# Latent attention: TensorE takes a pair's products in a written order, the plain fp32 ones together

## The chip, the cores and the metric

The kernel runs on one core of a Trainium2 chip. The metric is the device time of one execution in microseconds (us), lower is better. All engines of the core work at once, each in its own instruction order, and wait for one another through semaphores: TensorE (PE in the profile; PEld is its loading of weights), VectorE (DVE), ScalarE (ACT), GpSimd (POOL) and SyncE (SP), which here issues the loads.

## The reference

A trunk of two layers over 256 tokens of width 2048. The first mixes tokens by a gated product within chunks, the second by latent attention; both attend to 256 memory tokens beside it and end in a gated ConvFFN. The change lies in the latent attention of the second layer. Cut to what matters, for a block of 128 query positions:

```python
qa = jnp.einsum('bqhn,rhn->bqhr', qn, w_uk)
s = (jnp.einsum('bqhr,bkr->bhqk', qa, c_kv)
     + jnp.einsum('bqhp,bkp->bhqk', qr, k_rope)).astype(jnp.float32) * scale
s = jnp.where(k_pos[None, :] <= q_pos[:, None], s, -jnp.inf)
p = jax.nn.softmax(s, axis=-1).astype(c_kv.dtype)
o_lat = jnp.einsum('bhqk,bkr->bqhr', p, c_kv)
return jnp.einsum('bqhr,rhv->bqhv', o_lat, w_uv)
```

There are 12 heads. A score is the sum of a product over 128 "nope" dimensions and one over 64 rotary dimensions; the first query block sees 128 keys and the second 256. A value product follows the softmax, and then the output projection `w_out`, which also takes the four heads of memory attention.

## The kernel before

**Number formats.** Most products keep fp32 accuracy in three fp32r products: an operand is split into a high part (an fp32r copy by ACT) and a low part (the difference, by DVE), and `three` (lines 600 to 604) multiplies high by high, low by high and high by low. Where both operands are used plainly, one fp32 product is issued instead. In the profile an fp32 product of 128x128 weights shows as two matmul records, an fp32r product as one; a transposition of a 128x128 block is one record, on plain fp32 data too.

**Stages.** `layer_b` builds the latent tiles, then the value tiles of all heads (`vh`, `vl` split, `v1` plain), and then walks through six pairs of heads in the loop at line 1296. Round i makes the queries and keys of pair i (`queries`, `keys`: fp32r, weights split from `raw` into `whi` by ACT and `wlo` by DVE) and gives the rotary part to POOL (`rotary`, tiles `rm`, `rn`, then `qr` split by ACT and DVE). It then takes, in the program's text:

- `turn` for both heads of pair i-2: three transpositions of the probabilities `p` each, into one PSUM tile; ACT and DVE split the first 256 columns into `pT` (high, low) and ACT copies the last 128 into `pl`;
- `mturn` for a memory head: four transpositions;
- `scores` for pair i-1: for each query block (`qb` 0 with 128 keys, 1 with 256) one PSUM bank, into which three fp32r rotary products (`krz`, `qr`; both heads side by side) and then the two heads' fp32 products (`qn` and `kn`, which lie in `scratch`) are summed; `softmax` follows on DVE and ACT for each head;
- `attend` for both heads of pair i-2: three fp32r products of `pT` and `exact`, one fp32 product of `pl` and `scratch`, and a split of the result into `mainhl`;
- `mout` and `mscores` for memory heads, fp32r throughout (`mpT`, `rest`, `exact`).

The last pair's scores, and the transpositions and value products of the last two pairs, stand as hooks between chunks of `w_out`'s first quarter (`hooks`, line 1318). Below, round i is one pass of that loop, and the first and second head are the two of its pair i-2.

**What sets the order.** The program is built with a scheduler that moves instructions on each engine by a timeline of its own; the text above is its input, not its result. A block of code under `manual_schedule(engines=...)` keeps its instructions in written order on the engines it names; before the change, this part has none. PSUM tiles come from one pool of eight banks (`psum`), so that a new tile waits until the readers of the tile that last had its bank are done. All loads go through SP's queue in program order.

Of the kernel before, what the change touches and what calls it, by code (L numbers as in the profile page):

```python
# [16 lines left out]
P = 128  # L17
D = 2048
S = 256
# [55 lines left out]
class Kernel:  # L75
# [1003 lines left out]
    def layer_b(self):  # L1079
# [9 lines left out]
        with tc.tile_pool(name="lb", bufs=1) as lb:  # L1089
# [138 lines left out]
            def scores(pr):  # L1228
                bank = [self.psum() for _ in range(2)]
                for qb in range(2):  # L1230
                    n = P * (qb + 1)
                    q = [qr[pr][:, i * S + qb * P : i * S + (qb + 1) * P] for i in range(2)]
                    both = bank[qb][:, : 2 * n].rearrange("p (j k) -> p j k", j=2)
                    self.three(both, q, [k[:, :, :n] for k in krz], True, False)
                    for j in range(2):
                        mm(both[:, j, :], qn[pr][:, j, qb * P : (qb + 1) * P], kn[pr][:, j, :n], start=False, stop=j == 1)  # L1236
                for j in range(2):
                    softmax(2 * pr + j, [bank[qb][:, j * P * (qb + 1) : (j + 1) * P * (qb + 1)] for qb in range(2)])
# [21 lines left out]
            def turn(h):  # L1260
# [4 lines left out]
                pT, last = self.tmp(lp, [P, 576], "pT", 2, F32R)[:, 13 : 13 + 512], self.tmp(lp, [P, P], "pl", 2)  # L1265
                self.split(pT, acc[:, :S])
                nc.scalar.activation(last, acc[:, S : 3 * P], AF.Copy)
                pa[h] = pT, last

            def attend(h):  # L1270
                pT, last = pa.pop(h)
                o = self.psum()
                cols = slice(h * P, (h + 1) * P)
                self.three(o[:, :S], (vh[:, cols], vl[:, cols]), (pT[:, :S], pT[:, S:]), True, False)
                mm(o[:, P:S], v1[:, cols], last, start=False, stop=True)
                self.split(hl[:, h, :], o[:, :S])
# [280 lines left out]
```

## Time and profile before

| | |
|---|---|
| median of 3 runs | 2030.38 us (2029.91 to 2031.34) |
| span of the profiled execution, first to last instruction | 2027.8 us |
| granted TensorE clock, mean | 0.999 |
| PE busy | 2017.2 us (99%) |
| DVE busy | 1618.2 us (80%) |
| ACT busy | 1167.1 us (58%) |
| POOL busy | 112.8 us (6%) |
| chain that ended last, by engine | PE 99% |

The page gives the span of the profiled execution and no device time of its own beside it; the timed runs of the same kernel lie 2.1 to 3.5 us above that span, the median 2.58 us. Starts are counted from the beginning of the span. The latent attention's pairs stand between about 1163 and 1243 us of it. In the timeline a row is one instruction or a run of equal ones: its start, its length, the engine, line, operation, output and inputs, shape and count, and in brackets the idle time just before it and what ended it. Matmuls are pipelined, so their lengths overlap, and the distance between the starts of neighbours tells how fast PE goes.

### The profile page before, as it was taken

How to read it: one execution, taken by the hardware profiler on the slowest of the kernel's cores; microseconds unless marked ns; L12 is line 12 of the kernel's file. 1: busy time of each engine (PE TensorE's matmuls, PEld its weight loads, DVE VectorE, ACT ScalarE, POOL GpSimd, SP SyncE). 2: the span in 40 equal slices, each digit the busy share in tenths (PEclk: the TensorE clock that was granted, in tenths of full speed). 3: DMA queues.
4: the chain of work that ended last, by engine and by line, in shares of the span. 5: the costliest groups of instructions: out<-in, count | busy, mean ns of one | idle time of the engine just before them, and what ended most of it. 6: DMA issues, size and time to landing. Idle time of an engine off the chain costs nothing.

```text
span 2027.8 us, 38053 instructions
## 1 busy us (share of the span) xinstructions
PE 2017.2 (99%) x15136; PEld 1912.3 (94%) x15136; DVE 1618.2 (80%) x2433; ACT 1167.1 (58%) x1675; POOL 112.8 (6%) x169
## 2 busy tenths in 40 slices
PE   9999999999999999999999999999999999999998
PEld 8989999999889999899989999999988999889996
DVE  6866766778898788987878786777889878898787
ACT  6754744545565555655566675455566555565565
POOL 0000013100000000000002141400000000000000
PEclk9999999999999999999999999999999999999999
DMA  8876556688657676577656634568865767657764
GB/s 255 234 216 181 166 193 195 192 209 259 208 177 218 198 240 199 179 216 246 187 179 187 183 113 162 190 196 210 257 205 181 219 192 246 196 177 219 241 206 145
DMA packets 248263, 409.24 MB, mean 202 GB/s; under 512 B 71502, under 2 KB 78996, under 8 KB 248084
## 3 DMA queue, kind: packets, MB, share of 16 engines
q1 hardware_dynamic: 247892, 406.27, 65.4%
q8 instruction: 118, 1.93, 0.4%
q14 instruction: 61, 0.50, 0.1%
q10 hardware_dynamic: 192, 0.54, 0.1%
HBM read 400.46 MB, written 2.10 MB: 199 GB/s over the span
## 4 chain that ended last, share of the span: by engine, by line
PE 99%; DVE 0%; ACT 0%; issue 0%; ACTq 0%
PE ps L157 22%; PE ps L158 22%; PE ps L160 22%; PE ps L796 7%; PE ps L797 7%; PE ps L795 7%; PE ps L189 2%; PE ps L190 2%; PE ps L191 2%; PE ps L524 1%; PE ps L406 0%; PE ps L604 0%; PE ps L602 0%; PE ps L603 0%; PE ps L1236 0%; PE ps L1024 0%
## 5 line engine op out<-in xcount | busy, mean ns | idle before, releaser
L118 ACT ACTIVATE whi<-raw 128x1024 fp32r<-128x1024 f32 x484 | 512.7, 1061 | 513.1 <-PE ps L158 373.6
L119 DVE TENSOR_TENSOR wlo<-raw,whi 128x1024 fp32r<-128x1024 f32 x484 | 599.0, 1241 | 246.6 <-ACT whi L118 244.1
L157 PE MATMUL ps<-xhl,whi 128*128 128x256 f32 x3264 | 763.1, 277 | 0.0
L158 PE MATMUL ps<-xhl,whi 128*128 128x256 f32 x3264 | 761.5, 276 | 0.0
L158 PEld LDWEIGHTS ps<-xhl,whi 128*128 128x128 f32 x3264 | 612.8, 188 | 0.5
L157 PEld LDWEIGHTS ps<-xhl,whi 128*128 128x128 f32 x3264 | 612.7, 188 | 0.6
L160 PE MATMUL ps<-xhl,wlo 128*128 128x256 f32 x3264 | 436.6, 276 | 0.0
L160 PEld LDWEIGHTS ps<-xhl,wlo 128*128 128x128 f32 x3264 | 400.5, 188 | 0.0
L710 DVE TENSOR_TENSOR wlo<-raw,whi 128x1024 fp32r<-128x1024 f32 x112 | 134.3, 1220 | 31.5 <-ACT whi L709 30.3
L796 PE MATMUL ps<-wlo,h 128*128 128x512 f32 x404 | 157.3, 390 | 0.0
L797 PE MATMUL ps<-whi,h 128*128 128x512 f32 x404 | 157.2, 389 | 0.0
L709 ACT ACTIVATE whi<-raw 128x1024 fp32r<-128x1024 f32 x112 | 115.7, 1055 | 53.1 <-PE ps L158 37.3
L795 PE MATMUL ps<-whi,h 128*128 128x512 f32 x404 | 128.8, 390 | 0.0
L157 PE MATMUL ps<-mainhl,whi 128*128 128x256 f32 x512 | 119.7, 277 | 0.0
L158 PE MATMUL ps<-mainhl,whi 128*128 128x256 f32 x512 | 119.3, 276 | 0.0
L890 ACT ACTIVATE c<-a,cT 128x256 f32<-128x256 f32 x176 | 99.7, 592 | 32.2 <-DVE a L237 30.2
L709 ACT ACTIVATE whi<-xs 128x1024 fp32r<-128x1024 f32 x52 | 53.8, 1059 | 87.3 <-DVE xs L757 73.1
L158 PEld LDWEIGHTS ps<-mainhl,whi 128*128 128x128 f32 x512 | 96.0, 188 | 0.0
L157 PEld LDWEIGHTS ps<-mainhl,whi 128*128 128x128 f32 x512 | 95.9, 188 | 0.0
L795 PEld LDWEIGHTS ps<-whi,h 128*128 128x128 f32 x404 | 75.8, 188 | 15.7
L797 PEld LDWEIGHTS ps<-whi,h 128*128 128x128 f32 x404 | 75.8, 188 | 15.7
L796 PEld LDWEIGHTS ps<-wlo,h 128*128 128x128 f32 x404 | 75.9, 188 | 15.4
(378 smaller groups left out, 2896.6 us busy)
## 6 DMA issues: line engine op xcount, KB each, us to landing
raw<-in_w_ffn_up SPq DMA_DIRECT2D x352, 512.0 KB, 4.4
raw<-in_w_ffn_down SPq DMA_DIRECT2D x126, 512.0 KB, 4.5
raw<-in_w_out SPq DMA_DIRECT2D x64, 512.0 KB, 3.9
raw<-in_w_in_a SPq DMA_DIRECT2D x56, 512.0 KB, 4.2
gate<-in_w_ffn_down SPq DMA_DIRECT2D x38, 512.0 KB, 4.6
raw<-in_w_mem_kv SPq DMA_DIRECT2D x31, 512.0 KB, 4.8
sums<-in_w_ffn_down SPq DMA_DIRECT2D x48, 256.0 KB, 7.1
raw<-in_w_in_b SPq DMA_DIRECT2D x16, 512.0 KB, 4.1
```

What stands on the lines that cost most here:

```text
L118: nc.scalar.activation(hi[:, :n], raw[:, :n], AF.Copy)
L119: nc.vector.tensor_tensor(lo[:, :n], raw[:, :n], hi[:, :n].bitcast(F32), ALU.subtract)
L157: mm(acc[:, :S], wh, x[:, :S], start=first, stop=False)
L158: mm(acc[:, :S], wh, x[:, S:], start=False, stop=False)
L160: mm(acc[:, :S], wl, x[:, :S], start=False, stop=last)
L189: mm(acc, xh, wh, start=first, stop=False)
L709: self.behind(self.nc.scalar.activation(hi, w, AF.Copy))
L710: self.behind(self.nc.vector.tensor_tensor(lo, w, hi.bitcast(F32), ALU.subtract))
L795: mm(o, xh, wh, start=start, stop=False)
L796: mm(o, xh, wl, start=False, stop=False)
L797: mm(o, xl, wh, start=False, stop=stop)
L890: nc.scalar.activation(c, a, AF.Identity, scale=w(2), bias=w(3))
```

## The change

It does four things. `scores` writes the four fp32 products of a pair first, for both query blocks, and the six rotary fp32r products behind them. `turn` copies `pl` before it splits `pT`. `attend` takes two heads: both heads' three fp32r products, then both fp32 products, then both splits. And in the loop, `turn`, `mturn`, `scores` and `attend` stand in one block that keeps PE in written order; `mout` and `mscores` stand outside it, and so do the hooks, whose `scores` and `attend` calls are only passed another way.

```diff
             def scores(pr):
                 bank = [self.psum() for _ in range(2)]
+                both = [bank[qb][:, : 2 * P * (qb + 1)].rearrange("p (j k) -> p j k", j=2) for qb in range(2)]
                 for qb in range(2):
                     n = P * (qb + 1)
+                    for j in range(2):
+                        mm(both[qb][:, j, :], qn[pr][:, j, qb * P : (qb + 1) * P], kn[pr][:, j, :n], start=j == 0, stop=False)
+                for qb in range(2):
                     q = [qr[pr][:, i * S + qb * P : i * S + (qb + 1) * P] for i in range(2)]
-                    both = bank[qb][:, : 2 * n].rearrange("p (j k) -> p j k", j=2)
-                    self.three(both, q, [k[:, :, :n] for k in krz], True, False)
-                    for j in range(2):
-                        mm(both[:, j, :], qn[pr][:, j, qb * P : (qb + 1) * P], kn[pr][:, j, :n], start=False, stop=j == 1)
+                    self.three(both[qb], q, [k[:, :, : P * (qb + 1)] for k in krz], False, True)
...
                 pT, last = self.tmp(lp, [P, 576], "pT", 2, F32R)[:, 13 : 13 + 512], self.tmp(lp, [P, P], "pl", 2)
+                nc.scalar.activation(last, acc[:, S : 3 * P], AF.Copy)
                 self.split(pT, acc[:, :S])
-                nc.scalar.activation(last, acc[:, S : 3 * P], AF.Copy)
                 pa[h] = pT, last
 
-            def attend(h):
...
+            def attend(*heads):
+                outs = [(h, self.psum(), slice(h * P, (h + 1) * P), *pa.pop(h)) for h in heads]
+                for h, o, cols, pT, last in outs:
+                    self.three(o[:, :S], (vh[:, cols], vl[:, cols]), (pT[:, :S], pT[:, S:]), True, False)
+                for h, o, cols, pT, last in outs:
+                    mm(o[:, P:S], v1[:, cols], last, start=False, stop=True)
+                for h, o, *_ in outs:
+                    self.split(hl[:, h, :], o[:, :S])
...
+                with tc.manual_schedule(engines={mybir.EngineType.PE}):
+                    if i >= 2:
+                        turn(2 * i - 4)
+                        turn(2 * i - 3)
+                        mturn(i - 2)
+                    if i >= 1:
+                        scores(i - 1)
+                    if i >= 2:
+                        attend(2 * i - 4, 2 * i - 3)
                 if i >= 2:
-                    turn(2 * i - 4)
-                    turn(2 * i - 3)
-                    mturn(i - 2)
-                if i >= 1:
-                    scores(i - 1)
-                if i >= 2:
-                    attend(2 * i - 4)
-                    attend(2 * i - 3)
                     mout(i - 2)
...
-                2: calls(attend, pairs[0]),
+                2: [lambda: attend(*pairs[0])],
                 3: calls(turn, pairs[1]),
-                5: calls(attend, pairs[1]),
+                5: [lambda: attend(*pairs[1])],
```

No instruction is added or removed on any engine, and SP's and POOL's orders stay as they were. Line numbers shift: a pair's fp32 score product is L1236 before and L1234 after, a head's transposition L1264 and L1265, its fp32 value product L1275 and L1276.

The first place is PE in round 2, from the transpositions to the value products. `ident,p` are the heads' transpositions and `ident,mp` the memory head's; `krz,qr` are the rotary products, `scratch` alone the fp32 score products, `pT,exact` the value products in fp32r and `pl,scratch` those in fp32; a number behind a name is the tile's. Before:

```order
L645 MATMUL ps_13848<-ident,mp_13713 128x128 x4
L602 MATMUL ps_13856<-krz_12346,qr_13626 128x256
...
L604 MATMUL ps_13856<-krz_12347,qr_13626 128x256
L1236 MATMUL ps_13856<-scratch 128x128 x2
L602 MATMUL ps_13857<-krz_12346,qr_13626 128x512
...
L1236 MATMUL ps_13857<-scratch 128x256 x2
L602 MATMUL ps_13888<-pT_13834,exact 128x256
L603 MATMUL ps_13888<-pT_13834,exact 128x256
L602 MATMUL ps_13895<-pT_13843,exact 128x256
L603 MATMUL ps_13895<-pT_13843,exact 128x256
L604 MATMUL ps_13888<-pT_13834,exact 128x256
...
L1275 MATMUL ps_13888<-pl_13835,scratch 128x128
```

And with the change:

```order
L645 MATMUL ps_13856<-ident,mp_13719 128x128 x4
L1234 MATMUL ps_13864<-scratch 128x128 x2
L1234 MATMUL ps_13865<-scratch 128x256 x2
L602 MATMUL ps_13864<-krz_12346,qr_13629 128x256
...
L604 MATMUL ps_13864<-krz_12347,qr_13629 128x256
L602 MATMUL ps_13865<-krz_12346,qr_13629 128x512
...
L602 MATMUL ps_13896<-pT_13842,exact 128x256
L603 MATMUL ps_13896<-pT_13842,exact 128x256
L604 MATMUL ps_13896<-pT_13842,exact 128x256
L602 MATMUL ps_13897<-pT_13851,exact 128x256
...
L1276 MATMUL ps_13896<-pl_13843,scratch 128x128
L1276 MATMUL ps_13897<-pl_13852,scratch 128x128
```

The fp32 score products moved up to the transpositions, and the two fp32 value products stand next to each other. The first head's third value product (L604, which reads the low part of `pT`) moved from fifth to third of the value products, ahead of the second head's first two.

The second place is PE in `w_out`'s first quarter, where the last pair's scores stand (`mainhl,whi` and `mainhl,wlo` are `w_out`'s products). Before, the scores of the two query blocks follow each other:

```order
L1236 MATMUL ps_14561<-scratch 128x128 x2
L602 MATMUL ps_14562<-krz_12346,qr_14401 128x512
L603 MATMUL ps_14562<-krz_12346,qr_14401 128x512
L604 MATMUL ps_14562<-krz_12347,qr_14401 128x512
L1236 MATMUL ps_14562<-scratch 128x256 x2
```

With the change, this is where the second bank begins:

```order
L1234 MATMUL ps_14579<-scratch 128x128 x2
L602 MATMUL ps_14579<-krz_12346,qr_14416 128x256
...
L604 MATMUL ps_14579<-krz_12347,qr_14416 128x256
L157 MATMUL ps_14545<-mainhl_13326,whi_14630 128x256
...
L157 MATMUL ps_14548<-mainhl_13326,whi_14630 128x256
...
L1234 MATMUL ps_14580<-scratch 128x256 x2
...
L1265 MATMUL ps_14611<-ident,p_14502 128x128 x3
```

Between the two banks stand now twelve products of `w_out` (the first and the last are shown), and the second bank's products come ahead of the transpositions instead of following the first bank at once. The second bank (`ps_14562` before, `ps_14580` after) takes the place in PSUM of a value product's output of round 5 (`ps_14504` before, `ps_14521` after), eight tiles earlier, and waits until that one is split.

The third place is DVE in round 5, which makes the low part of that split (`mainhl`); `md` and `p` belong to the softmax of pair 4. Before:

```order
L1250 TENSOR_SCALAR md_14494<-md_14494 128x2
L246 TENSOR_TENSOR mainhl_13326<-ps_14504,mainhl_13326 128x256
L1255 RECIPROCAL md_14484<-md_14484 128x2
...
L1257 TENSOR_SCALAR p_14495<-p_14495,md_14494 128x256
L246 TENSOR_TENSOR mainhl_13326<-ps_14511,mainhl_13326 128x256
```

And with the change:

```order
L1251 TENSOR_SCALAR md_14511<-md_14511 128x2
L1256 RECIPROCAL md_14501<-md_14501 128x2
...
L1258 TENSOR_SCALAR p_14512<-p_14512,md_14511 128x256
L246 TENSOR_TENSOR mainhl_13326<-ps_14521,mainhl_13326 128x256
L246 TENSOR_TENSOR mainhl_13326<-ps_14522,mainhl_13326 128x256
```

The first head's split moved from ahead of the softmax's last steps to behind them, and ACT's high part moved likewise. Over the whole attention, PE goes from a plain fp32 instruction (a product or a transposition) to an fp32r one 30 times before and 15 times after: in round 1 two and one, in each of rounds 2 to 5 five and two, in the hooks eight and six.

More of the change, by code (lines that the diff above doesn't have):

```diff
@@ L1265, in turn @@
                 pT, last = self.tmp(lp, [P, 576], "pT", 2, F32R)[:, 13 : 13 + 512], self.tmp(lp, [P, P], "pl", 2)
+                nc.scalar.activation(last, acc[:, S : 3 * P], AF.Copy)
                 self.split(pT, acc[:, :S])
-                nc.scalar.activation(last, acc[:, S : 3 * P], AF.Copy)
                 pa[h] = pT, last
-            def attend(h):
[L1271 to L1276, printed above, removed]
+            def attend(*heads):
[6 more added lines that the diff above has]
+                    self.split(hl[:, h, :], o[:, :S])
             parts = {}
```

## The prediction

> **What bounds the kernel.** I read the page first, then the list of what PE waited for, then a table by stage, and last the timelines of PE, DVE and ACT in the latent attention.
>
> ```profile
> span 2027.8 us, 38053 instructions
> PE 99%; DVE 0%; ACT 0%; issue 0%; ACTq 0%
> ```
>
> ```profile
> PE ps L491 <- DVE ones L288: 1.1, 1, 1.1
> PE ps L604 <- DVE pT L246: 0.2, 1, 0.2
> PE ps L796 <- DVE wlo L710: 0.2, 1, 0.2
> ```
>
> ```profile
> core 0: us, PE busy (x) PEld busy (x) DVE busy (x) ACT busy (x) POOL busy (x), PEclk, DMA share, GB/s
> 1174.12:1180.59 6.47, 6.31 (x49) 5.85 (x48) 6.24 (x17) 4.37 (x13) 4.64 (x6) 1.00 0.67 199
> 1187.40:1193.63 6.23, 6.23 (x49) 5.86 (x48) 6.20 (x17) 4.06 (x13) 4.72 (x6) 1.00 0.62 211
> 1200.43:1206.46 6.03, 6.03 (x49) 5.79 (x47) 4.74 (x13) 3.57 (x10) 5.13 (x6) 1.00 0.70 233
> ```
>
> The first fence says that the chain which ended last is PE throughout; the second, that PE's list of waits in 2027.8 us holds 1.5 us. A gain can only come from PE work that takes longer than it must, a loss only from a wait on PE that isn't there yet. The third shows the part of rounds 2, 3 and 4 that the change rewrites (transpositions to memory products), with equal work: 6.47, 6.23 and 6.03 us, at full clock. The two slower ones are those in which DVE was busy nearly throughout (6.24 and 6.20 us, against 4.74).
>
> **What a change from plain fp32 to fp32r costs.** This is what the change saves, 15 times of 30. PE in round 2:
>
> ```profile
> 1174.12 0.82 PE L1264 MATMUL ps<-ident,p 128*128 128x128 f32 x6
> 1174.77 0.60 PE L645 MATMUL ps<-ident,mp 128*128 128x128 f32 x4
> 1175.13 0.37 PE L602 MATMUL ps<-krz,qr 128*128 128x256 f32 x1
> 1175.33 0.28 PE L603 MATMUL ps<-krz,qr 128*128 128x256 f32 x1
> 1175.45 0.28 PE L604 MATMUL ps<-krz,qr 128*128 128x256 f32 x1
> ...
> 1176.72 1.02 PE L1236 MATMUL ps<-scratch 128*128 128x256 f32 x4
> 1177.39 0.47 PE L602 MATMUL ps<-pT,exact 128*128 128x256 f32 x1
> 1177.70 0.28 PE L603 MATMUL ps<-pT,exact 128*128 128x256 f32 x1
> 1177.83 0.29 PE L602 MATMUL ps<-pT,exact 128*128 128x256 f32 x1
> 1177.95 0.28 PE L603 MATMUL ps<-pT,exact 128*128 128x256 f32 x1
> 1178.39 0.38 PE L604 MATMUL ps<-pT,exact 128*128 128x256 f32 x1 [0.16 <-DVE pT L246]
> 1178.61 0.28 PE L602 MATMUL ps<-mpT,rest 128*128 128x256 f32 x1
> ```
>
> The first fp32r product behind plain fp32 looks dear: 1175.13 to 1175.33 is 0.20 us, where its neighbour takes 0.12, and 1177.39 to 1177.70 is 0.31 us, against 0.13. But the whole run says otherwise. Six transpositions take 1174.77 - 1174.12 = 0.65 us, 0.108 each, so ten end at 1174.12 + 1.08 = 1175.20; with 0.12 for the first rotary product the next would start at 1175.32, and it starts at 1175.33. For fp32 products over 256 columns I choose 0.215 a record, twice the 0.108 of 128 columns: four from 1176.72 end at 1177.58, and 1177.58 + 0.12 = 1177.70 is where the next stands. So the long record is only the place where the profile starts it early, and a change of format costs 0 to 0.01 us. The other end is the record as it stands: 0.08 to 0.09 us behind 128 columns, which is what all 15 saved ones follow (each round still has one behind a 256-column product). **15 x 0.01 = 0.15 us at most by the sums, 15 x 0.085 = 1.3 us by the records.** I take the sums, as they close twice to 0.01.
>
> The Trainium skill, "FP8 and Floating Point Precision", TensorE Precision Notes, says that true fp32 takes four passes through the array, and names no cost for what stands beside it. Read so, nothing is saved by gathering such products; the 0.01 above agrees.
>
> **The first head's third product comes too early.** It reads the low part of `pT`, and that is DVE's:
>
> ```profile
> L246 DVE TENSOR_TENSOR pT<-ps,pT x12: 408/415/419, 1177.9 to 1235.7; 128x256 fp32r<-128x256 f32 x12
> ```
>
> ```profile
> 1176.09 1.92 DVE L115 TENSOR_TENSOR wlo<-raw,whi 128x512 fp32r<-128x512 f32 x2
> 1177.93 0.74 DVE L246 TENSOR_TENSOR pT<-ps,pT 128x256 fp32r<-128x256 f32 x2
> ```
>
> ```profile
> 1190.96 0.74 DVE L246 TENSOR_TENSOR pT<-ps,pT 128x256 fp32r<-128x256 f32 x2
> ```
>
> ```profile
> 1191.23 0.28 PE L603 MATMUL ps<-pT,exact 128*128 128x256 f32 x1
> 1191.42 0.39 PE L604 MATMUL ps<-pT,exact 128*128 128x256 f32 x1
> ```
>
> ```profile
> 1203.11 0.74 DVE L246 TENSOR_TENSOR pT<-ps,pT 128x256 fp32r<-128x256 f32 x2
> ```
>
> ```profile
> 1204.62 0.28 PE L604 MATMUL ps<-pT,exact 128*128 128x256 f32 x1
> ```
>
> The group's row (shortest, median and longest in ns) gives a low part 0.41 us, so the first of the two that start at 1177.93 is done at 1178.34; L604 starts at 1178.39. Without the wait it would have started 0.12 behind its neighbour, at 1178.07: a stall of 0.32 us, more than the 0.16 of the bracket, which counts from the end of the modelled record. Its own slot is then 1178.61 - 1178.39 = 0.22 instead of 0.12: **a wait costs 0.10 us beside itself.** In round 3, 1191.42 - 1191.23 = 0.19 is 0.07 of stall. With the change L604 stands two products of 0.12 earlier, and DVE's order ahead of it is the same, so that it is done no sooner: the two products then come behind the wait instead of before it. Round 2 loses **0.24 us**.
>
> The first two products hide only while ACT's high part comes in time, and `pl` now stands ahead of it:
>
> ```profile
> 1176.78 0.68 ACT L245 ACTIVATE pT<-ps 128x256 fp32r<-128x256 f32 x2
> ...
> 1178.37 0.61 ACT L1267 ACTIVATE pl<-ps 128x128 f32<-128x128 f32 x2 [0.43 <-DVE pT L246]
> ```
>
> One `pl` takes at most 0.61 / 2 = 0.30, and a high part is done some 0.4 behind its start, so the first ends at 1177.5 instead of 1177.2; the products behind it start by the sums at 1177.58, and DVE takes the low part only from 1177.93, behind its weights. That costs nothing. Queued behind the waiting L604 on PE are the second head's products and the memory ones, nobody else's input before the next round.
>
> Is round 3 another 0.24? That hangs on whether DVE and ACT follow PE there. They don't, as I read it:
>
> ```profile
> 1181.01 0.42 ACT L245 ACTIVATE qr<-rm 128x256 fp32r<-128x256 f32 x1 [2.03 <-POOL rm L1135]
> ```
>
> ACT waits 2.03 us for POOL's rotation, which was started before the wait in question, and goes on from there with no long gap until round 3's `pT`. So DVE ends round 3's low part at the same moment as before, PE, already 0.24 late, waits less, and behind round 3 it is still 0.24 late, not 0.48. In round 4 the low part is done at 1203.11 + 0.41 = 1203.52, and L604 moves from 1204.62 four products forward to about 1204.14: no wait, with 0.6 us to spare.
>
> **The last scores wait for their second bank.** PE and DVE there before:
>
> ```profile
> 1221.40 0.28 PE L602 MATMUL ps<-krz,qr 128*128 128x256 f32 x1
> 1221.51 0.28 PE L603 MATMUL ps<-krz,qr 128*128 128x256 f32 x1
> 1221.62 0.28 PE L604 MATMUL ps<-krz,qr 128*128 128x256 f32 x1
> 1221.74 0.60 PE L1236 MATMUL ps<-scratch 128*128 128x128 f32 x4
> ```
>
> ```profile
> 1220.94 0.41 DVE L246 TENSOR_TENSOR mainhl<-ps,mainhl 128x256 fp32r<-128x256 f32 x1
> 1222.01 0.17 DVE L1255 RECIPROCAL md<-md 128x2 f32<-128x2 f32 x1 [0.66 <-ACT p L1252]
> ...
> 1223.55 0.75 DVE L246 TENSOR_TENSOR mainhl<-ps,mainhl 128x256 fp32r<-128x256 f32 x2
> ```
>
> ```profile
> 1220.00 0.42 ACT L245 ACTIVATE qr<-rm 128x256 fp32r<-128x256 f32 x1 [2.82 <-POOL rm L1135]
> ```
>
> The bank was free at 1220.94 + 0.41 = 1221.35, ahead of its use at 1222.10 or so. With the change this split stands where the later two stood, so it ends at 1223.55 + 0.41 = 1223.96; again by POOL's time, since ACT waited 2.82 us for it. L604 stood 0.05 behind the split it waited for, so the bank is open at 1224.01. PE would begin it after 4 x 0.108 for fp32, 3 x 0.115 for rotary and 12 x 0.113 for `w_out` behind 1221.40: 1221.40 + 0.43 + 0.35 + 1.36 = 1223.54. The wait ends 0.47 later, and its 0.10 comes on top: **PE is 0.57 us late.** That isn't added to the 0.24: the release is POOL's, so a PE that is late already waits less. Queued behind are the pair's other products, two heads' transpositions and `w_out`; what is transposed there is used two chunks of `w_out` later. In rounds 1 to 5 the scores' banks were last the queries', which ACT copies out well before.
>
> The Trainium skill, "TensorE: Matmul & The Clock Gate", Step-by-step, says that PE pulls weight loads ahead of matmuls in flight. By it a waiting matmul would have its weights already and the 0.10 would fall away, for a sum of +0.47; the row's 0.22-us slot behind the wait speaks against that here, and the row decides.
>
> **The sum** on the profiled execution: up to the bank's release +0.57, with both earlier terms swallowed, since PE there starts from POOL's time; behind it, the two format changes that are saved there (0.02 at most). 2027.8 + 0.57 - 0.02 = 2028.35 us of span. The median lies 2030.38 - 2027.8 = 2.58 above the profiled span, which I keep: **2030.9 us.**
>
> **Rivals.**
>
> - *The records are right* and a change of format costs 0.085 us. Thirteen are saved before the bank, 1.1 us, but PE then waits for it until 1224.01 whatever it saved; only the two behind count, 0.17. Unless the release moves with PE too: then -1.3 + 0.57 = -0.7, 2029.7 us. Against it: the sums that close. Chance 0.14.
> - *The waits don't come*, because DVE's and ACT's queues run sooner, and only the sums' gain is left: -0.15, 2030.2 us. For it: the split's new place is a scheduler's, and DVE idles 0.66 us right behind the old one. Chance 0.17.
> - *Slower: DVE's low part is late in every pair.* The place is L604 of each first head, six times; the price is what round 2 would show, two products more than 0.32 of stall, 0.56, and 0.10: 0.66 each. Less what stands before (0.42 and 0.17), with the bank's 0.57: 6 x 0.66 - 0.59 + 0.57 = +3.9, 2034.3 us. It decides from the point where the low part ends later than 1204.14 in round 4, 0.6 us later than before, as when `pl` and the softmax push ACT back. Chance 0.06, half of it beyond 0.2% with the spread of runs.
> - *The delays add up*, since ACT and DVE follow PE: 2 x 0.24 + 0.57 = +1.05, 2031.4 us. Chance 0.15.
> - That the change doesn't do what it says is no rival: the order shows the 15 that are left.
>
> **How the numbers follow.** The forecast, +0.2 to +0.9, has 0.48. All but the slow rival lie within 0.2% of the time, 4.1 us, which is about what a measurement of this kernel can tell from no change: same 0.94, slower 0.04 and faster 0.02 for a release or a cost that no row shows. The range takes in the first rival's 2029.7 and the added delays' 2031.4, and at each end the spread of the three runs, 0.5 below and 1.0 above their median: 2029.2 to 2032.4.
>
> **What would show it.** The first fp32r record behind plain fp32 stays long, in 15 places, and the sums over such runs stay the same. L604 of the first head in round 2 starts at about 1178.4 with a wait of 0.5 us behind the product ahead of it, none in rounds 4 and 5. L1234's second bank in `w_out` waits for DVE's `mainhl` until about 1224.0. If the part from 1163 to 1243 us is shorter than before, the cost of a change of format is real and I am wrong; if it is over 2 us longer, the waits are.

## The result and the profile after

The changed kernel takes **2045.57 us** (median of 5 runs, 2045.21 to 2045.93) against 2029.91 us before (2029.41 to 2031.34): 1.0075 times as long, with a 95% interval of 1.0063 to 1.0087. It is 15.66 us slower where a loss of half a microsecond was forecast, and lies 13 us above the range.

This is the list of what PE waits for now, over the whole execution:

```profile
PE ps L491 <- DVE ones L288: 1.1, 1, 1.1
PE ps L157 <- ACT mainhl L245: 0.4, 1, 0.4
PE ps L604 <- DVE pT L246: 0.4, 1, 0.4
PE ps L330 <- DMA graw<-in_g_mem: 0.2, 1, 0.2
PE ps L796 <- DVE wlo L710: 0.2, 1, 0.2
```

These are 2.3 us, 0.8 more than before. So some 15 us are lost without a wait. The table by stage tells where. First the kernel before, over the three quarters of `w_out` that follow the attention and the beginning of the ConvFFN:

```profile
core 0: us, PE busy (x) PEld busy (x) DVE busy (x) ACT busy (x) POOL busy (x), PEclk, DMA share, GB/s
1243.00:1300.00 57.00, 57.00 (x505) 57.00 (x505) 42.05 (x45) 27.14 (x33) 21.32 (x23) 1.00 0.55 182
1300.00:1360.00 60.00, 60.00 (x529) 59.95 (x529) 42.52 (x56) 32.87 (x41) 7.67 (x8) 1.00 0.67 201
1360.00:1420.00 60.00, 60.00 (x532) 60.00 (x531) 45.02 (x69) 30.39 (x39) 0.00 (x0) 1.00 0.82 208
1420.00:1480.00 60.00, 60.00 (x532) 60.00 (x531) 52.21 (x81) 35.23 (x47) 0.00 (x0) 1.00 0.80 252
```

And the changed kernel, in the same stretches:

```profile
1243.00:1300.00 57.00, 57.00 (x477) 57.00 (x476) 38.55 (x45) 25.60 (x33) 18.59 (x21) 1.00 0.52 179
1300.00:1360.00 60.00, 60.00 (x501) 59.95 (x500) 41.48 (x48) 30.15 (x36) 10.31 (x11) 1.00 0.58 184
1360.00:1420.00 60.00, 60.00 (x502) 60.00 (x502) 42.29 (x65) 28.78 (x39) 0.00 (x0) 1.00 0.79 204
1420.00:1480.00 60.00, 60.00 (x502) 60.00 (x502) 50.87 (x81) 32.54 (x42) 0.00 (x0) 1.00 0.73 239
```

PE is busy throughout in both, at the full granted clock (1.00), and what it does here is not touched by the change. But it gets through 477 products where it got through 505, and 502 where it got through 532: 57.00 / 505 = 0.113 us each before, 57.00 / 477 = 0.120 us now. The busy share can't show this, since it is full either way; the count beside it does. The group's durations say the same (shortest, median and longest in ns, 1243 to 1500 us), before and then after:

```profile
L157 PE MATMUL ps<-xhl,whi x512: 276/276/467, 1311.8 to 1485.3; 128*128 128x256 f32 x171
```

```profile
L157 PE MATMUL ps<-xhl,whi x505: 282/283/470, 1318.0 to 1499.9; 128*128 128x256 f32 x169
```

The shortest is now 282 ns, 6 above the median before. The timeline of PE shows where it begins, at the first pair's value products in `w_out`:

```profile
1231.86 0.28 PE L602 MATMUL ps<-pT,exact 128*128 128x256 f32 x1
1231.98 0.28 PE L603 MATMUL ps<-pT,exact 128*128 128x256 f32 x1
1232.10 0.28 PE L604 MATMUL ps<-pT,exact 128*128 128x256 f32 x1
1232.22 0.61 PE L1276 MATMUL ps<-pl,scratch 128*128 128x128 f32 x4
1232.58 0.36 PE L157 MATMUL ps<-mainhl,whi 128*128 128x256 f32 x1
1232.78 0.28 PE L158 MATMUL ps<-mainhl,whi 128*128 128x256 f32 x1
1232.90 0.28 PE L157 MATMUL ps<-mainhl,whi 128*128 128x256 f32 x1
1233.03 0.28 PE L158 MATMUL ps<-mainhl,whi 128*128 128x256 f32 x1
1233.14 0.28 PE L157 MATMUL ps<-mainhl,whi 128*128 128x256 f32 x1
```

and where it ends, at the ConvFFN's first products of 512 columns:

```profile
1501.67 0.28 PE L158 MATMUL ps<-xhl,whi 128*128 128x256 f32 x1
1501.79 1.12 PE L160 MATMUL ps<-xhl,wlo 128*128 128x256 f32 x8
1502.75 0.40 PE L795 MATMUL ps<-whi,h 128*128 128x512 f32 x1
```

Up to there eight products take 1502.75 - 1501.79 = 0.96 us, 0.120 each; from there on PE is as fast as before. Between 1232.6 and 1502.75 us the trace has 2240 records of 256 columns; at 120.0 instead of 113.3 ns they are worth 2240 x 6.7 ns = 14.9 us.

The same product can be looked up in both traces (the k-th of a line with the same tiles), and the difference of the two starts is how far PE is behind:

| until | PE is behind by | added here |
|---|---|---|
| 1163 us, ahead of every changed instruction | 0.62 us | 0.62, the start-up, which varies from run to run (-0.40 to +1.77 in those below) |
| end of round 2 | 0.90 us | 0.28: 0.02 in round 1, 0.26 at the first head's L604 |
| last scores, before | 0.91 us | 0.01 |
| last scores, behind | 1.62 us | 0.71, a wait in `w_out`'s first chunks |
| 1502.75 us | 16.34 us | 14.72, the slower pace |
| end | 16.35 us | 0.01 |

Without the start-up it is 15.7 us, which is what the medians show.

The time from one start on PE to the next is called a slot here. These are the slots in ns, computed from the starts in the two traces, with a bar where the kind of product changes; hook 2 and hook 5 are the first and the second pair's value products in `w_out`:

```
before, hook 5:   values 123 117 123 | fp32 109 30 | values 201 124 119 | fp32 114 28 | w_out 205 120 117 122 118 118 119 113 113 114
changed, hook 2:  values 123 117 123 117 123 120 | fp32 109 110 112 31 | w_out 199 122 120 120 120 120 ...
changed, hook 5:  values 117 123 120 117 123 120 | fp32 109 110 112 31 | w_out 199 122 120 120 120 120 ...
```

Before, PE comes back from plain fp32 with slots of 117 to 122 too, but after six of them it drops to 113. In the changed kernel the third slot is 120, and so are nearly all that follow. The rows of before from which its last slots come:

```profile
1241.00 0.37 PE L157 MATMUL ps<-mainhl,whi 128*128 128x256 f32 x1
1241.21 0.28 PE L158 MATMUL ps<-mainhl,whi 128*128 128x256 f32 x1
1241.33 0.28 PE L157 MATMUL ps<-mainhl,whi 128*128 128x256 f32 x1
...
1242.04 0.28 PE L157 MATMUL ps<-mainhl,whi 128*128 128x256 f32 x1
1242.15 0.28 PE L158 MATMUL ps<-mainhl,whi 128*128 128x256 f32 x1
1242.26 0.28 PE L157 MATMUL ps<-mainhl,whi 128*128 128x256 f32 x1
```

### The profile page after: what moved, and what is told of

The parts are those of the page before. It is cut to its first block, busy times and chain, and to the rows that moved or that the text cites. A ratio compares the mean times of both kernels' runs of the same rounds, so it can differ in the third digit from the quotient of the medians.

```text
span 2044.2 us, 38069 instructions
## 1 busy us (share of the span) xinstructions
PE 2032.6 (99%) x15136; PEld 1927.5 (94%) x15136; DVE 1619.5 (79%) x2433; ACT 1165.0 (57%) x1675; POOL 112.6 (6%) x169
## 4 chain that ended last, share of the span: by engine, by line
PE 98%; ACT 1%; DVE 0%; POOL 0%; issue 0%; DMA 0%; ACTq 0%
PE ps L157 22%; PE ps L158 22%; PE ps L160 22%; PE ps L796 7%; PE ps L797 7%; PE ps L795 7%; PE ps L189 2%; PE ps L190 2%; PE ps L191 2%; PE ps L524 1%; PE ps L406 0%; PE ps L604 0%; PE ps L602 0%; PE ps L603 0%; PE ps L1024 0%; PE ps L1234 0%
## 5 line engine op out<-in xcount | busy, mean ns | idle before, releaser
L157 PE MATMUL ps<-mainhl,whi 128*128 128x256 f32 x512 | 122.1, 280 | 0.4 <-ACT mainhl L245 0.4
L158 PE MATMUL ps<-mainhl,whi 128*128 128x256 f32 x512 | 121.8, 279 | 0.0
```

Of the source, the lines that this page charges most:

```text
L157: mm(acc[:, :S], wh, x[:, :S], start=first, stop=False)
L158: mm(acc[:, :S], wh, x[:, S:], start=False, stop=False)
```

## The experiments

Theory: a pace of 120 ns that keeps itself up, entered by the pairs' order in the hooks of `w_out`. Rivals: four plain fp32 records in a row do it (A); another part of the change, or another engine, slows PE (B). In the tables behind the quoted expectations, "120s" counts `w_out` and ConvFFN products of 119.5 to 120.5 ns behind 1225 us. One run each, unless an interval is given; the kernel before took 2029.75 to 2031.23 us beside them.

**The heads apart again, in the hooks alone**

```diff
-                2: [lambda: attend(*pairs[0])],
+                2: calls(attend, pairs[0]),
...
-                5: [lambda: attend(*pairs[1])],
+                5: calls(attend, pairs[1]),
```

> The changed kernel, with the two hooks of w_out that work out a pair's values calling each head by itself again, as before. Theory: PE falls into a slower rhythm (120 ns instead of 113 from one 128x256 product to the next) behind the pair's fp32 products at 1232.6 us, and the rhythm repeats itself until the first 512-wide products at 1502.8 us, 2240 products times 6.7 ns = 14.9 us. With the heads apart no slot should stay at 120: about 2030.9 us, the changed kernel's 2045.6 less 14.7. Rival A, four plain fp32 records in a row are what does it, whatever stands ahead of them: the same 2030.9 here. Rival B, the slower pace comes from another part of the change (later splits on ACT and DVE, the scores' waits, the order in the rounds) or from contention with other engines: 2045.6, unchanged.

**The pairs alone, in the kernel before**

```diff
-                2: calls(attend, pairs[0]),
+                2: [lambda: attend(*pairs[0])],
...
-                5: calls(attend, pairs[1]),
+                5: [lambda: attend(*pairs[1])],
```

(with the new `attend`)

> The kernel before, with only the two hooks of w_out changed so that a pair's value products stand together and their fp32 products behind them; rounds, scores and transpositions as before. Theory: the lead-in and the fp32 run are the same as in the changed kernel, so PE locks at 120 ns again: 2029.9 + 14.9 = about 2044.8 us. Rival A (four fp32 records in a row): the same. Rival B (another part of the change): about 2030, no slot stays at 120.

The first took 2030.46 us, the second 2043.75 us, with 2173 slots of 120 and nothing else of the change in it. From 1243 to 1300 us PE does 505 products in the first:

```profile
1243.00:1300.00 57.00, 57.00 (x505) 57.00 (x504) 41.27 (x46) 27.14 (x33) 21.33 (x23) 1.00 0.54 178
```

and in the second:

```profile
1243.00:1300.00 57.00, 57.00 (x477) 57.00 (x476) 39.43 (x44) 26.02 (x32) 20.66 (x23) 1.00 0.52 175
```

So the two hooks hold the whole loss of pace: the rounds, the scores and the split's new place in the rounds play no part in it. What is left of B is that in the hooks, too, both splits come later on ACT and DVE.

**One more product behind the fp32 ones**, 512 or 256 columns wide, its result unread

```diff
                 for h, o, cols, pT, last in outs:
                     mm(o[:, P:S], v1[:, cols], last, start=False, stop=True)
+                if heads[0] >= 8:
+                    mm(self.psum()[:, :512], vh[:, cols], pT[:, :512], start=True, stop=True)
```

> The changed kernel, with one more fp32r product of 512 columns, whose result nobody reads, behind the fp32 products of a pair in the two hooks of w_out. Theory: a 512-wide product is what ended the 120-ns rhythm at 1502.8 us, so it ends it here too, at the cost of 2 x 0.23 us: 2030.9 + 0.5 = about 2031.4 us. If the rhythm is set by something that lasts (buffers, addresses, other engines), it comes back behind the product: 2045.6 + 0.5 = 2046.1 us.

> As the run with a 512-wide product behind a pair's fp32 products, but with the extra product only 256 wide: same operands, same place, nobody reads it. Theory: only the longer stream of 512 columns gives PE the time to fall back, since 256-wide products follow each other in the 120-ns rhythm by thousands; the rhythm stays: 2045.6 + 2 x 0.12 = about 2045.8 us. Rival, any product put between the fp32 run and w_out shifts the moment of coming back and so frees PE: about 2031.1 us.

2031.12 us with 512 columns, 2030.97 with 256, no lasting 120 in either. The first agrees with the theory; the second refutes what I added to it, that only a longer stream frees PE. A product of either width put between was enough. Both runs keep the hooks' later splits, so these don't slow PE either, and B is out.

**The pair's fp32 products a chunk later**

```diff
-                2: [lambda: attend(*pairs[0])],
-                3: calls(turn, pairs[1]),
-                5: [lambda: attend(*pairs[1])],
+                2: [lambda: values_of(*pairs[0])],
+                3: [lambda: rest_of(*pairs[0])] + calls(turn, pairs[1]),
+                5: [lambda: values_of(*pairs[1])],
+                6: [lambda: rest_of(*pairs[1])],
```

(`values_of` issues the `three` of each head, `rest_of` the fp32 products and splits)

> The changed kernel, with a pair's two fp32 products (still next to each other, four records in a row) put off in both hooks of w_out by one chunk of w_out, so that 113-ns products stand ahead of them instead of the values' 117 to 123 ns. Theory: the lead-in sets the phase in which PE comes back from plain fp32; behind 113-ns products all such runs of this kernel faded back to 113 within ten products, so about 2030.9 us. Rival A (four fp32 records in a row do it, whatever stands ahead): PE locks, about 2045 us.

2034.07 us, with 1.8 us of it this run's start-up, 0.9 a new wait for `whi`, and 41 slots of 120. These stand where nobody expected them, ahead of the fp32 products. PE's timeline:

```profile
1233.32 0.28 PE L604 MATMUL ps<-pT,exact 128*128 128x256 f32 x1
1233.44 0.28 PE L157 MATMUL ps<-mainhl,whi 128*128 128x256 f32 x1
1233.56 0.28 PE L158 MATMUL ps<-mainhl,whi 128*128 128x256 f32 x1
1233.68 0.28 PE L157 MATMUL ps<-mainhl,whi 128*128 128x256 f32 x1
1233.80 0.28 PE L158 MATMUL ps<-mainhl,whi 128*128 128x256 f32 x1
1233.92 0.28 PE L157 MATMUL ps<-mainhl,whi 128*128 128x256 f32 x1
1234.04 0.28 PE L158 MATMUL ps<-mainhl,whi 128*128 128x256 f32 x1
```

There is no plain fp32 in between, and PE goes at 0.12 a product. The next plain fp32 ended it, four records of products and six transpositions in a row. So A is wrong: fp32 isn't needed to enter the pace.

**One head's three products straight ahead of `w_out`**

```diff
-                2: [lambda: attend(*pairs[0])],
-                3: calls(turn, pairs[1]),
-                5: [lambda: attend(*pairs[1])],
+                2: [lambda: values_of(8)],
+                3: [lambda: values_of(9)] + calls(turn, pairs[1]),
+                4: [lambda: rest_of(8, 9)],
+                5: calls(attend, pairs[1]),
```

> The changed kernel, with the first pair's value products one head (three products) at a time, each straight ahead of w_out's products with no plain fp32 behind it, the pair's fp32 products a chunk later, and the second pair's heads apart as before. When both heads' six value products stood straight ahead of w_out (the run with the fp32 products put off), PE went to 120 ns with no fp32 in between. Theory: it takes six of them, since three end before the 117 and 123 ns have settled to 120, so no slot stays at 120 here: 2030.9 us and up to 1 us for a later split. Rival, passing from value products to w_out's does it by itself: runs of 24 or more slots of 120 behind 1232 us, and 2031 to 2045 us by what ends them.

**Seven value products in place of six**

```diff
+                if heads[0] >= 8:
+                    mm(self.psum()[:, :S], vh[:, cols], pT[:, :S], start=True, stop=True)
                 for h, o, cols, pT, last in outs:
                     mm(o[:, P:S], v1[:, cols], last, start=False, stop=True)
```

> The changed kernel with one more 128x256 value product, whose result nobody reads, ahead of a pair's fp32 products in the hooks of w_out: seven in place of six. Theory: PE locks when it comes back from the fp32 run at one certain moment (first slot of 199 or 200 ns); behind seven products this moment is another, so the slots fade to 113 within ten products: about 2031.2 us. Rival, many value products and fp32 in a row are enough whatever the moment: a lock again, about 2045.8 us.

**The second hook's heads apart, the first one's together**

```diff
-                5: [lambda: attend(*pairs[1])],
+                5: calls(attend, pairs[1]),
```

> The changed kernel with the second hook's pair by heads apart as before; the first hook's pair stays together. Theory: PE locks at 1232.6 us as in the changed kernel; if the lock passes through the old order of value and fp32 products, as it passed through six transpositions, the time is again about 2045 us; if the old order ends it at about 1243 us, 90 products times 6.7 ns = 0.6 us are lost and the time is about 2031.4 us. Rival, each hook is needed or adds its share: about 2038 us.

| | us | 120s | slots behind the value products, ns |
|---|---|---|---|
| three, no fp32 | 2031.79 | 25 | w_out 117 118 122 120 120 120 ..., ended by six transpositions |
| six, no fp32 (the run above) | 2034.07 | 41 | w_out 117 118 122 120 120 120 ..., ended by fp32 and transpositions |
| six, fp32, one value product (256 wide) | 2030.97 | 0 | fp32 109 110 112 31, value 201, w_out 116 121 122 118 119 118 113 |
| seven, fp32 | 2031.29 | 0 | fp32 113 110 112 31, w_out 199 113 114 113 |
| six and fp32 in the first hook alone | 2030.78 | 66 | first hook as in the changed kernel; ended by the second hook |

It isn't the number of value products: three are enough, and my theory of six is refuted. It isn't the first slot of 199 ns either, which came with seven and led straight to 113. What is left: behind value products (slots of 117 to 123) PE may come back to `w_out` in either pace, and a run of plain fp32 keeps the slow one or ends it. The slots just ahead differ by a nanosecond or two; that these differences decide isn't shown. Nor do four fp32 records in a row slow PE by themselves: in the first run of the table they stand between products of 113 ns, and the slots behind them go 205 118 117 121 119 118 118 114. Before, in the last hook, each head's three products were followed by two fp32 records, and PE dropped back; it did so behind all other runs of that kernel too. The last row shows which hook costs what: the first one's 120s were ended by the second hook's old order at 1242 us, so that nearly all of the 14.7 us come by the second hook, behind which nothing but products of 256 columns follows for 260 us. The pairs alone in the kernel before say the same: there the first hook's 120s ended at six transpositions at 1234 us, through which they passed in the changed kernel, and 14.2 us were lost behind the second hook.

**The value products' operand from another place**

```diff
-                pT, last = self.tmp(lp, [P, 576], "pT", 2, F32R)[:, 13 : 13 + 512], self.tmp(lp, [P, P], "pl", 2)
+                pT, last = self.tmp(lp, [P, 576], "pT", 2, F32R)[:, :512], self.tmp(lp, [P, P], "pl", 2)
```

> The changed kernel, with the tile of transposed probabilities read from its first element on instead of its 13th; same instructions, same order. Theory: the 117 and 123 ns of the value products come from where their operands lie in SBUF against each other, so their slots change here, and with them the moment at which w_out's products follow; if the 120 goes, about 2030.9 us. Rival, the place plays no part and the order alone does it: the same slots of 117 and 123, the same lock, 2045.6 us.

2030.97 us and no lasting 120. The six value slots were 121 113 116 124 120 120 instead of 123 117 123 117 123 120, so the place of an operand counts, with every instruction and its order unchanged. But this also moved the moment of coming back, so it doesn't say what the second pace is. Two runs of the kernel before asked that directly, by shifting the split weights that PE loads (those that stream through it already lie at element 0):

```diff
-        return w[:, :1024] if moves else w[:, 19 : 19 + 1024]
+        return w[:, :1024] if moves else w[:, :1024]
```

(and 16)

> The kernel before, with the split weight tiles (high and low) read from their first element on instead of their 19th; same instructions, same order. It asks what the two paces of 113 and 120 ns are. Theory: PE reads the next weights from SBUF while it streams the moving operand, and where the two lie against each other sets the pace; at another place the 11880 products of 256 columns on split weights run at another pace throughout, 120 ns for instance: 2029.9 + 11880 x 6.7 ns = about 2109 us. Rival, the place plays no part, and 120 ns is only a disturbed start that keeps itself up: 2029.9 us, and slots of 113.

> The kernel before, with the split weight tiles read from their 16th element on instead of their 19th, 64 bytes behind the first. Theory as for the run from the first element; if what counts is where the operands lie within 64 bytes, this run is as long as that one, and if within a longer period, it differs. Rival, the place plays no part: 2029.9 us.

2108.39 us from element 0: 78.5 us more than the 2029.87 before it, where 11880 x 6.7 ns = 79.6 us was expected. Nearly every slot is 120 there. And 2063.36 us from element 16, where PE goes in two paces again, by stretches: 113.3 ns from 1263 us to the end of the products of 256 columns at about 1510, 117.8 ns in those behind 1590 us. Then the changed kernel at four more places:

```diff
-        return w[:, :1024] if moves else w[:, 19 : 19 + 1024]
+        return w[:, :1024] if moves else w[:, 8 : 8 + 1024]
```

(and 24, 35, 51)

> The changed kernel with the split weight tiles read from their 8th element on instead of their 19th. Of the places seen, 0 gives 120 ns throughout, 16 a mean of 117 and 19 gives 113, with 120 possible once PE has been put on it. Estimate by that: a place nearer to 0 than to 19 has the slow pace as its own, 2045 to 2110 us; a place at which only one pace of 113 exists would give about 2031 us, the pair order kept.

> The changed kernel with the split weight tiles read from their 24th element on. If the place sets which paces exist, one beyond 19 and further from 0 may hold 113 ns without a second pace: about 2031 us, the pair order kept. If 19 is the only good one, 2045 us or more. If a faster pace than 113 exists there, below 2030 us.

> The changed kernel with the split weight tiles read from their 35th element on, 64 bytes behind the 19th. The runs at 0 and 16, also 64 bytes apart, differed by 45 us, so that 64 bytes are not the period; no lock: about 2031 us; a lock as at 19: 2045 us; the slow pace throughout: 2110 us.

> The changed kernel with the split weight tiles read from their 51st element on, 128 bytes behind the 19th. If the places repeat every 128 bytes, it does what 19 does: 113 ns, then the lock at 120 from the pairs in w_out on, about 2045.6 us. If they don't repeat, anything from 2030 to 2110 us.

| weights from element | kernel | us | mean start to start, ns (9734 `xhl` products) |
|---|---|---|---|
| 19 | before | 2029.91 | 113.4 |
| 19 | changed | 2045.57 | 114.4 (113 and 120) |
| 16 | before | 2063.36 | 116.3 |
| 0 | before | 2108.39 | 120.0 |
| 24 | changed | 2082.51 | 117.8 |
| 8 | changed | 2089.26 | 118.3 |
| 35 | changed | 2089.57 | 118.6 |
| 51 | changed | 2128.03 | 121.9 |

The group's row in the run from element 0, over the whole execution, has the changed kernel's slow median of 283 ns for all of it:

```profile
L157 PE MATMUL ps<-xhl,whi x3264: 277/283/469, 168.8 to 2032.1; 128*128 128x256 f32 x192
```

and the run from element 51 is slower still:

```profile
L157 PE MATMUL ps<-xhl,whi x3264: 278/287/469, 168.9 to 2051.7; 128*128 128x256 f32 x192
```

Within each of the two kernels these runs have the same instructions, order and clock, and PE's waits in them add up to at most 2.2 us: another place of the weights alone changes PE's pace, and places 64 or 128 bytes apart don't repeat. None of the six other places keeps 113 ns throughout, and none of these runs beats either kernel. The place doesn't fix the pace by itself: at element 19 both 113 and 120 are possible, at element 16 both 113.3 and 117.8. At 19, the runs above show that what came just before decides.

**What the waits came from**

> The changed kernel with the heads apart in w_out's hooks (2030.46 us in its run) and, in the first hook, the last pair's scores bank by bank as before; the rounds stay changed. It shows what the wait for the second bank is worth. Theory: of the 1.0 us by which PE is later at 1228 us beside the start-up, 0.7 is this wait, so PE is 0.7 us earlier behind the scores than with the heads apart alone: about 2029.8 us. Rival, the lag comes from the rounds and is only passed on: 2030.5 us, no change.

2031.21 us, and the 0.71 us at the last scores stayed (0.73): the theory falls, the scores' order isn't what PE waits for there. The next run took the pairs apart in the rounds too, and left all else of the change:

```diff
-                        attend(2 * i - 4, 2 * i - 3)
+                        attend(2 * i - 4)
+                        attend(2 * i - 3)
```

> The changed kernel with each head's fp32 product behind its own value products in the rounds too, not in the hooks alone; the written order on PE, the scores' order and the early copy for the last product stay. ACT's list then has the split of the first head's result ahead of the next softmax again. Theory: the 0.7 us that PE loses at the last scores comes from that split, which in the changed kernel stands behind the softmax together with two more, and w_out's products wait for the last of them; here the lag from 1220 to 1226 us is below 0.1, and the time about 2030.5 - 0.7 = 2029.8 us, if the first wait in round 2 (0.27) stays. Rival, the scores' new order is what makes PE wait there: 0.7 stays, 2030.5 us.

2030.32 us, ratio 1.0003 (0.9994 to 1.0013). PE is behind by 0.26 us more after round 2, gets 0.2 back in round 3, and loses 0.02 at the last scores: the wait is gone. ACT's timeline shows why. In this run, as before the change, one split of a head's result stands ahead of the softmax (L1253) and two behind it:

```profile
1220.16 0.42 ACT L245 ACTIVATE qr<-rm 128x256 fp32r<-128x256 f32 x1 [3.15 <-POOL rm L1135]
1220.49 0.37 ACT L245 ACTIVATE mainhl<-ps 128x256 fp32r<-128x256 f32 x1
...
1222.92 0.62 ACT L245 ACTIVATE mainhl<-ps 128x256 fp32r<-128x256 f32 x2
```

In the changed kernel all three stand behind it, and the last ends at 1223.68 + 0.90 = 1224.58:

```profile
1220.92 0.42 ACT L245 ACTIVATE qr<-rm 128x256 fp32r<-128x256 f32 x1 [3.15 <-POOL rm L1135]
...
1223.68 0.90 ACT L245 ACTIVATE mainhl<-ps 128x256 fp32r<-128x256 f32 x3
```

PE's product of that block starts at 1224.63:

```profile
1223.92 0.28 PE L158 MATMUL ps<-mainhl,whi 128*128 128x256 f32 x1
1224.63 0.73 PE L157 MATMUL ps<-mainhl,whi 128*128 128x256 f32 x4 [0.44 <-ACT mainhl L245]
1225.20 1.02 PE L1234 MATMUL ps<-scratch 128*128 128x256 f32 x4
```

**Scores and copy alone** (the loop and the hooks as before, only `scores` and `turn` changed)

> The changed kernel with rounds and hooks as before (heads apart, no written order on PE); only the scores' new order (fp32 products of both banks first) and the early copy for the last product are left of the change. Theory: these two cost nothing that shows, and gain nothing: within 0.3 us of the kernel before, no wait of 0.4 at the last scores. Rival, the gathered scores save their changes of format, 12 of them at 0.085 us: 1 us less than before.

2029.70 us, ratio 1.0000 (0.9991 to 1.0010); between 1168 and 1510 us PE goes from 0.18 to 0.21 us ahead, a gain of 0.03 us. The rival's count in the expectation was wrong: this run goes from plain fp32 to fp32r 21 times instead of 30, nine fewer and not twelve, so by 0.085 us each it would have gained 0.77. The trace shows a small part of that.

## Why the prediction was wrong

*What a change of format costs: right.* 0 to 0.01 us each was the forecast; the run with scores and copy alone gains 0.03 us for nine, rounds 3 to 5 of the changed kernel gain nothing for nine (PE is 0.90 us behind ahead of them, 0.91 at their end), and the long first record is still there (1232.58 to 1232.78).

*The first head's third product: right in place, cause and size.* 0.24 us was forecast for round 2, 0.26 was added, with the wait of 0.4 at L604, released by DVE's `pT`:

```profile
1178.34 0.28 PE L603 MATMUL ps<-pT,exact 128*128 128x256 f32 x1
1179.04 0.39 PE L604 MATMUL ps<-pT,exact 128*128 128x256 f32 x1 [0.42 <-DVE pT L246]
```

Without the start-up's 0.62 it starts at 1178.42, where 1178.4 was forecast. Rounds 3 to 5 added 0.01 us, as forecast.

*`pl` ahead of `pT`: right*, nothing, by the run with scores and copy alone.

*The last scores: the place right, the rest not.* Forecast were 0.57 us, for the second bank, released at POOL's time whatever PE had lost before, so that the 0.24 would be swallowed. Measured are 0.71 us, on top of the 0.29. PE doesn't wait for the bank: a product of `w_out` ahead of it waits for ACT's split. And ACT's time there isn't the old one. In rounds 2 to 4 `qr` is split 0.65 or 0.64 us later than before, which is the start-up, though PE is 0.26 us further behind from round 2 on: up to there the release is POOL's, as the prediction says. In round 5 it is 0.92 us later (1220.92 against 1220.00), and the other 0.27 come from ACT's own order. Its third split now stands behind the softmax of round 4, all that follows on ACT is later by it, and so are the copies for which round 5's rotation waits (they start at 1213.98 instead of 1213.08). Behind round 5's softmax the same happens once more. That 0.92 is also what PE is behind (0.91) is chance: with the heads apart in the rounds `qr` is 0.16 later where PE is 0.59 behind. The rival "the delays add up" comes near in number, 1.05 us against 0.28 + 0.01 + 0.71 = 1.0, but not for its reason: its second 0.24 stayed away, and ACT didn't follow PE.

*The step that failed* stands under all the others and was never written down as one: every product that the change doesn't move was priced at the 0.113 us it took before ("12 x 0.113 for `w_out`"). By waits and formats alone the time would have been 2029.91 + 1.0 = 2030.9 us, and the runs with the heads apart (2030.46) or one more product between (2030.97) lie near it. That this is the very number of the forecast is luck: the forecast adds 0.55 to a median of 2030.38. The other 14.7 us are the pace of 2240 unmoved products. The sums over switches that closed to 0.01 us ended at the second product behind the switch; the rows that followed, which before the change stayed at 116 to 122 ns for six products in `w_out`, were in the trace and weren't read. And the last of the signs that were to show it, a part from 1163 to 1243 us over 2 us longer, looked for the loss in the wrong stretch: the second hook's first `w_out` product starts at 1243.04 instead of 1241.00, 1.4 us later without the start-up, and the rest is lost behind it.

Could the trace of before have shown it? Not that the pace would hold, since no head's products there were followed so. But it showed slots of 116 to 122 ns for the same products at full clock, so a second pace was possible, and nothing but products of 256 columns for 260 us behind the last hook. A rival "PE stays in the slower slots" would have been priced from those rows at some 2240 x 0.007 = 15.7 us; it was missing, and with it the upper end of the range.

What stays open is what in the chip makes the two paces. It is shown that the weights' place changes the pace, and that at element 19 the order of a few products decides between two paces. Which reads meet, and why 120 holds for thousands of products at element 19, was not taken apart: the weights' shift also moves what ACT and DVE write, and the trace shows starts only to a nanosecond.

## What to carry to other kernels

Where PE is full from end to end, compare products per microsecond stage by stage, not busy shares or waits: a loss of 6% stood in the counts (505 against 477), and neither in the busy shares nor in the waits. When a change puts other products ahead of a long run of equal ones, look at the slots of that run: the loss can lie behind the changed place and be fifteen times as large as all its waits. If it appears, another product between, or another order in the last place before the run, can end it, and the place of the weights in SBUF is worth a scan of its own.

## What the runs showed of the hardware

- Products of 128x256 in fp32r at the full granted clock have more than one steady pace: 113.3 and 120.0 ns from start to start. The slow one held for 2240 products, over changes of tiles, weights and PSUM banks, and through six transpositions at 1236 us; it ended at products of 512 columns, and in other runs at six transpositions or at plain fp32 products with others between or behind them. With the weights from element 16 the same products had paces of 113.3 and 117.8 ns, each for hundreds in a row.
- The Trainium skill, "TensorE: Matmul & The Clock Gate", Back-to-back issue gap, gives 262 cycles for 256 columns at the full clock of 2.4 GHz, as the gap of a product by itself. Worked out from that figure, 262 / 2.4 = 109 ns would be an estimate of one pace; the traces show 113 or 120. The same section says that the spacing in a stream of weight loads and products is set by both, pipelined. That the weights' place alone moves it from 113.4 to 120.0 ns in the kernel before (element 19 against 0) is compatible with that, but these runs don't show which part is slower.
- The Trainium skill, "SBUF — State Buffer", SBUF: two separate sides, says that PE never waits on anyone. PE's list of waits shows no more than before in the run from element 0 (1.3 us), but PE's pace depends on where the weights lie: 2029.9 us from element 19, 2108.4 from element 0.
